# Fewer, longer load runs and a last product that also sums the partial sums, in a streaming Poisson loss

## The chip, the cores and the metric

The kernel runs on one core of one Trainium2 chip. The metric is the device time of one execution in microseconds (us), median of several runs. All runs told of here were at a granted clock of 1.0. About 1.4 us of each time lies outside the span that the profile shows (84.78 against 83.4 for the profiled run of the kernel before).

## The reference

```python
# log_input, target: 1024 x 4096, float32
loss = np.exp(log_input) - target * log_input
return np.mean(loss, axis=-1)
```

33.55 MB are read and 4 KB written. A partition holds 8 consecutive rows of 4096 columns (16 KB a row), so 4 rows of one partition are 64 KB in one piece of memory.

## The kernel before

ScalarE takes the exp of x row by row and sums it, DVE multiplies t and x and sums that. All loads go out on one queue, x and t in turn: two rows (32 KB per partition) at a time for rows 0 to 5, row 6 alone, row 7 in seven pieces, so that little is left to compute after the last bytes. The first six loads are issued at once; the rest wait until the first pair of rows is done.

```python
TAIL = [("x", 32), ("t", 32), ("x", 24), ("t", 12), ("t", 12), ("x", 6), ("t", 5), ("x", 2), ("t", 3)]
...
for g in range(groups - 1):                       # groups = 4
    loads += [("x", 2 * d * g, 2 * d), ("t", 2 * d * g, 2 * d)]
...
# ScalarE, after its last exp: join the six partial sums of row 7
join(2 * n_whole, n_parts, most, len(t_work) - 1).then_inc(join_done, 1)
...
    nc.vector.wait_ge(landed[x_load], 16)
    nc.vector.tensor_tensor_reduce(               # the last one: accum_out = rest
        out=t_buf[...], in0=t_buf[...], in1=x_buf[...], op0=ALU.mult, op1=ALU.add, accum_out=accum, ...
    ).wait_op(landed[i], 16, "sem-ge").then_inc(prod_done, 1)
nc.vector.wait_ge(join_done, nb)
nc.vector.tensor_tensor(                          # the closing sum
    out=all_loss[:, nb - 1 : nb], in0=most, in1=rest, op=ALU.add
).wait_op(prod_done, len(t_work), "sem-ge").then_inc(loss_done, 1)
nc.sync.dma_start(out=out_v, in_=all_loss).wait_op(loss_done, 1, "sem-ge")...
```

## Time and profile before

| | before |
|---|---|
| time, median (range) | 84.19 us (84.17 to 84.25, 6 runs) |
| span of the profiled run | 83.4 us (its time: 84.78) |
| last load landed | 81.09 us |
| from there to the issue of the output | 0.81 us |
| from the output's issue to the end | 1.45 us |

The times count from the first issue of a load. The profiled run was 0.6 us slower than the timed ones; the slow packets that the prediction finds in its DMA records (its rival 2) are the likely reason. The lines of the page, of the table of stretches and of the timeline's end are shown in the prediction.

### The profile page before, as it was taken

Reading aid. Unit: us, or ns where it says so; the run is one execution under the profiler, and the core shown is the slowest. Engines: PE = TensorE matmul, PEld = TensorE weight load, DVE = VectorE, ACT = ScalarE, POOL = GpSimd, SP = SyncE. Lnnn points to the kernel's source line nnn. Section 1 sums busy time; section 2 is a strip of 40 time slices with the busy share of each in tenths; the row PEclk is TensorE's granted clock in tenths of the full one; section 3 lists DMA queues with packets and bytes.
Section 4 is the critical chain, followed back from the end, with each engine's and each line's share of the span. In section 5 each row is a group of like instructions: output and inputs, shape, how many; then the busy total and the mean of one; then the engine's idle time right before and its main releaser. Section 6 shows DMA issues by size and latency. Waiting matters only on the chain.

```text
span 83.4 us, 145 instructions
## 1 busy us (share of the span) xinstructions
DVE 35.9 (43%) x23; ACT 33.7 (40%) x37; POOL 0.2 (0%) x4
## 2 busy tenths in 40 slices
DVE  0000000000599960000099991000069995994992
ACT  0050029993001008998000102999300496019371
POOL 0000000000000000000000000000000000000000
DMA  8799969998996996995996997999799999999960
GB/s 252 330 425 503 487 283 487 503 409 346 503 503 252 503 503 252 503 503 252 503 503 267 487 503 330 425 503 440 314 448 432 409 472 387 430 407 422 395 224 2
DMA packets 2304, 33.56 MB, mean 403 GB/s; under 512 B 384, under 2 KB 640, under 8 KB 1152
## 3 DMA queue, kind: packets, MB, share of 16 engines
q1 hardware_dynamic: 2304, 33.56, 95.8%
HBM read 33.55 MB, written 0.00 MB: 403 GB/s over the span
## 4 chain that ended last, share of the span: by engine, by line
DMA 81%; DVE 7%; issue 6%; SPq 4%
DMA t_buf<-in_target_dram 81%; DVE t_buf L169 6%; SPq L114 4%; DVE parts L169 0%; DVE all_loss L180 0%; DVE rest L169 0%; SPq L113 0%
## 5 line engine op out<-in xcount | busy, mean ns | idle before, releaser
L169 DVE CUSTOM_DVE_ANT_0 t_buf<-t_buf,x_buf 128x4096 f32<-128x4096 f32 (+3 forms) x11 | 35.6, 3260 | 46.0 <-DMA t_buf<-in_target_dram 45.8
L139 ACT ACTIVATE e_dump<-x_buf 128x4096 f32<-128x4096 f32 (+3 forms) x10 | 29.0, 2901 | 23.3 <-DMA x_buf<-in_log_input_dram 23.1
L123 ACT ACTIVATE join_dump<-parts 128x2 f32<-128x2 f32 (+1 forms) x8 | 1.6, 204 | 20.5 <-DVE parts L169 20.2
L139 ACT ACT_TABLE_LOAD x1 | 1.3, 1283 | 4.0 <-PEq L48 4.0
L139 ACT ACTIVATION_READ_ACCUMULATOR e_dump<-x_buf 128x1 f32 x10 | 1.9, 186 | 0.0
L123 ACT ACTIVATION_READ_ACCUMULATOR join_dump<-parts 128x1 f32 x8 | 1.5, 186 | 0.0
L169 DVE DVE_READ_ACCUMULATOR2_ANT parts<- 128x1 f32 x10 | 0.8, 82 | 0.0
L180 DVE TENSOR_TENSOR all_loss<-most,rest 128x1 f32<-128x1 f32 x1 | 0.2, 159 | 0.0
L206 POOL MEMSET const-bfloat16-1.0<- 128x1 bf16 x1 | 0.1, 102 | 0.0
L206 POOL MEMSET const-uint8-127<- 128x1 uint8 x1 | 0.1, 101 | 0.0
L206 POOL MEMSET const-float32-0.0<- 128x1 f32 x1 | 0.1, 99 | 0.2 <-issue 0.2
L206 POOL MEMSET const-float32-1.0<- 128x1 f32 x1 | 0.1, 98 | 0.0
L169 DVE DVE_READ_ACCUMULATOR2_ANT rest<- 128x1 f32 x1 | 0.1, 82 | 0.0
## 6 DMA issues: line engine op xcount, KB each, us to landing
x_buf<-in_log_input_dram SPq DMA_DIRECT2D x3, 4096.0 KB, 30.6
t_buf<-in_target_dram SPq DMA_DIRECT2D x3, 4096.0 KB, 40.2
x_buf<-in_log_input_dram SPq DMA_DIRECT2D x1, 2048.0 KB, 35.5
t_buf<-in_target_dram SPq DMA_DIRECT2D x1, 2048.0 KB, 40.0
x_buf<-in_log_input_dram SPq DMA_DIRECT2D x1, 1536.0 KB, 43.2
t_buf<-in_target_dram SPq DMA_DIRECT2D x2, 768.0 KB, 45.3
x_buf<-in_log_input_dram SPq DMA_DIRECT2D x1, 384.0 KB, 46.5
t_buf<-in_target_dram SPq DMA_DIRECT2D x1, 320.0 KB, 46.6
```

Of the source, the lines that this page charges most:

```text
L114: dma = nc.sync.dma_start(out=buf[:, in_slot(lo, w)], in_=src[:, lo : lo + w])
L123: return nc.scalar.activation(out=join_dump[:, first : first + count], in_=parts[:, first : first + count], func=ACT_F.Copy, scale=inv_d, ...
L139: nc.scalar.activation(out=e_dump[:, col : col + w], in_=x_buf[:, in_slot(lo, w)], func=ACT_F.Exp, bias=0.0, scale=1.0, accum_out=parts[:, ...
L169: nc.vector.tensor_tensor_reduce(out=t_buf[:, in_slot(lo, w)], in0=t_buf[:, in_slot(lo, w)], in1=x_buf[:, in_slot(lo, w)], scale=-inv_d if ...
L180: nc.vector.tensor_tensor(out=all_loss[:, nb - 1 : nb], in0=most, in1=rest, op=ALU.add).wait_op(prod_done, len(t_work), "sem-ge").then_inc ...
L206: nc = _bacc.Bacc("TRN2", target_bir_lowering=False, num_devices=1)
```

## The change

Rows 0 to 3 of x go in one load of 64 KB per partition, then those of t; rows 4 and 5 keep 32 KB. That saves 2 loads and 16 packets for each DMA engine. The six partial sums of row 7 are laid behind the last columns of t, with -1 in the same places behind x, so that the last product, six columns wider, adds them up; the join on ScalarE and the closing sum go.

```diff
-    for g in range(groups - 1):
-        loads += [("x", 2 * d * g, 2 * d), ("t", 2 * d * g, 2 * d)]
+    for first, rows in ((0, 4), (4, 2), (6, 1)):
+        loads += [("x", first * d, rows * d), ("t", first * d, rows * d)]
...
+        if what == "x" and lo in (6 * d, 7 * d):          # buffers of rows 0 and 3 are used again
+            free = 1 if lo == 6 * d else 4
+            nc.sync.wait_ge(exp_done, free)
+            nc.sync.wait_ge(prod_done, free)
...
+    nc.gpsimd.memset(big["x"][:, 4 * d : 4 * d + n_parts], -1.0).then_inc(ones_done, 1)
...
-    join(2 * n_whole, n_parts, most, len(t_work) - 1).then_inc(join_done, 1)
...
+            nc.vector.wait_ge(ones_done, 1)
+            nc.vector.wait_ge(landed[i], 16)
+            nc.vector.wait_ge(prod_done, n_t - 1)
+            nc.vector.tensor_tensor_reduce(
+                out=place("t", lo, w + n_parts),
+                in0=place("t", lo, w + n_parts),
+                in1=place("x", lo, w + n_parts),
+                scale=-inv_d, ...
+                accum_out=all_loss[:, last_row : last_row + 1],
+            ).wait_op(exp_done, n_x, "sem-ge").then_inc(loss_done, 1)
-    nc.vector.wait_ge(join_done, nb)
-    nc.vector.tensor_tensor(
-        out=all_loss[:, nb - 1 : nb], in0=most, in1=rest, op=ALU.add
-    ).wait_op(prod_done, len(t_work), "sem-ge").then_inc(loss_done, 1)
```

More of the change, by code (lines that the diff above doesn't have):

```diff
@@ L8 @@
 F32 = mybir.dt.float32
-TAIL = [
-    ("x", 32), ("t", 32), ("x", 24), ("t", 12), ("t", 12), ("x", 6), ("t", 5), ("x", 2), ("t", 3),
-]
+TAIL = [("x", 24), ("t", 12), ("t", 12), ("x", 6), ("t", 5), ("x", 2), ("t", 3)]
 def before_first_barrier(nc, instructions):
@@ L54 @@
     inv_d = 1.0 / d
-    slots = 3
-    groups = nb // 2
+    last_row = nb - 1
     x_v = log_input.rearrange("(p b) d -> p (b d)", b=nb)
@@ L63 @@
     loads = []
-    for g in range(groups - 1):
-        loads += [("x", 2 * d * g, 2 * d), ("t", 2 * d * g, 2 * d)]
-    at = {"x": 2 * d * (groups - 1), "t": 2 * d * (groups - 1)}
+    for first, rows in ((0, 4), (4, 2), (6, 1)):
+        loads += [("x", first * d, rows * d), ("t", first * d, rows * d)]
+    at = {"x": last_row * d, "t": last_row * d}
     for what, w in TAIL:
@@ L81, with place, part @@
     x_work, t_work = work("x"), work("t")
-    n_whole = nb - 1
-    assert all(w == d for _, w, _ in x_work[:n_whole] + t_work[:n_whole])
-    x_buf = nc.alloc_sbuf_tensor("x_buf", [P, slots * 2 * d], F32).ap()
-    t_buf = nc.alloc_sbuf_tensor("t_buf", [P, slots * 2 * d], F32).ap()
-    e_dump = nc.alloc_psum_tensor("e_dump", [P, d], F32).ap()
-    n_parts = len(x_work) - n_whole + len(t_work) - n_whole - 1
-    parts = nc.alloc_sbuf_tensor("parts", [P, 2 * n_whole + n_parts], F32).ap()
-    join_dump = nc.alloc_sbuf_tensor("join_dump", [P, 2 * n_whole + n_parts], F32).ap()
-    most = nc.alloc_sbuf_tensor("most", [P, 1], F32).ap()
-    rest = nc.alloc_sbuf_tensor("rest", [P, 1], F32).ap()
+    n_x, n_t = len(x_work), len(t_work)
+    n_parts = n_x - last_row + n_t - last_row - 1
+    big = {
+        "x": nc.alloc_sbuf_tensor("x_big", [P, 4 * d + n_parts], F32).ap(),
+        "t": nc.alloc_sbuf_tensor("t_big", [P, 4 * d + n_parts], F32).ap(),
+    }
+    mid = {
+        "x": nc.alloc_sbuf_tensor("x_mid", [P, 2 * d], F32).ap(),
+        "t": nc.alloc_sbuf_tensor("t_mid", [P, 2 * d], F32).ap(),
+    }
+    def place(what, lo, w):
+        row = lo // d
+        if 4 <= row < 6:
+            return mid[what][:, lo - 4 * d : lo - 4 * d + w]
+        if row >= 6:
+            lo -= (6 if row == 6 else 4) * d
+        return big[what][:, lo : lo + w]
+    e_dump = nc.alloc_psum_tensor("e_dump", [P, d], F32).ap()
+    parts = nc.alloc_sbuf_tensor("parts", [P, 2 * last_row], F32).ap()
+    join_dump = nc.alloc_sbuf_tensor("join_dump", [P, 2 * last_row], F32).ap()
     all_loss = nc.alloc_sbuf_tensor("all_loss", [P, nb], F32).ap()
-    def in_slot(lo, w):
-        lo %= slots * 2 * d
-        return slice(lo, lo + w)
+    def part(k):
+        return big["t"][:, 4 * d + k : 4 * d + k + 1]
     landed = [nc.alloc_semaphore(f"landed{i}") for i in range(len(loads))]
@@ L103 @@
     join_done = nc.alloc_semaphore("join_done")
+    ones_done = nc.alloc_semaphore("ones_done")
     loss_done = nc.alloc_semaphore("loss_done")
@@ L109, with join @@
     for i, (what, lo, w) in enumerate(loads):
-        buf, src = (x_buf, x_v) if what == "x" else (t_buf, t_v)
-        if lo == 2 * d * slots and what == "x":
-            nc.sync.wait_ge(exp_done, 2)
-            nc.sync.wait_ge(prod_done, 2)
-        dma = nc.sync.dma_start(out=buf[:, in_slot(lo, w)], in_=src[:, lo : lo + w])
+        if what == "x" and lo in (6 * d, 7 * d):
+            free = 1 if lo == 6 * d else 4
+            nc.sync.wait_ge(exp_done, free)
+            nc.sync.wait_ge(prod_done, free)
+        src = x_v if what == "x" else t_v
+        dma = nc.sync.dma_start(out=place(what, lo, w), in_=src[:, lo : lo + w])
         dma.then_inc(landed[i], 16)
-        if lo + w <= 2 * d * slots:
+        if lo < 6 * d:
             early.append(dma.ins)
     before_first_barrier(nc, early)
-    def join(first, count, accum, prods):
+    nc.gpsimd.memset(big["x"][:, 4 * d : 4 * d + n_parts], -1.0).then_inc(ones_done, 1)
+    def join(row, exps):
         nc.scalar.wait_ge(exp_done, exps)
-        return nc.scalar.activation(
-            out=join_dump[:, first : first + count],
-            in_=parts[:, first : first + count],
+        nc.scalar.activation(
+            out=join_dump[:, 2 * row : 2 * row + 2],
+            in_=parts[:, 2 * row : 2 * row + 2],
             func=ACT_F.Copy,
             scale=inv_d,
-            accum_out=accum,
-        ).wait_op(prod_done, prods, "sem-ge")
-    exps = 0
-    for lo, w, i in x_work:
+            accum_out=all_loss[:, row : row + 1],
+        ).wait_op(prod_done, row + 1, "sem-ge").then_inc(join_done, 1)
+    for k, (lo, w, i) in enumerate(x_work):
         row, col = lo // d, lo % d
-        if row >= 2 and col == 0:
-            join(2 * (row - 2), 2, all_loss[:, row - 2 : row - 1], row - 1).then_inc(join_done, 1)
-        if col == 0 and row > 0:
-            nc.scalar.wait_ge(exp_done, exps)
-        k = 2 * row if row < n_whole else 2 * n_whole + exps - n_whole
+        if col == 0 and row >= 2:
+            join(row - 2, k)
+        elif col == 0 and row == 1:
+            nc.scalar.wait_ge(exp_done, k)
         nc.scalar.activation(
             out=e_dump[:, col : col + w],
-            in_=x_buf[:, in_slot(lo, w)],
+            in_=place("x", lo, w),
             func=ACT_F.Exp,
@@ L144 @@
             scale=1.0,
-            accum_out=parts[:, k : k + 1],
+            accum_out=parts[:, 2 * row : 2 * row + 1] if row < last_row else part(k - last_row),
         ).wait_op(landed[i], 16, "sem-ge").then_inc(exp_done, 1)
-        exps += 1
-        if row == n_whole and col == 0:
-            row -= 1
-            join(2 * row, 2, all_loss[:, row : row + 1], row + 1).then_inc(join_done, 1)
-    join(2 * n_whole, n_parts, most, len(t_work) - 1).then_inc(join_done, 1)
-    needs = {}
-    for lo, w, i in x_work:
-        needs[lo + w] = i
+        if col == 0 and row == last_row:
+            join(row - 1, k + 1)
@@ L157 @@
     for j, (lo, w, i) in enumerate(t_work):
         row = lo // d
-        last = j == len(t_work) - 1
-        if last:
-            accum = rest
-        elif row < n_whole:
-            accum = parts[:, 2 * row + 1 : 2 * row + 2]
-        else:
-            k = 2 * n_whole + len(x_work) - n_whole + j - n_whole
-            accum = parts[:, k : k + 1]
-        x_load = next(needs[end] for end in sorted(needs) if end >= lo + w)
-        nc.vector.wait_ge(landed[x_load], 16)
-        nc.vector.tensor_tensor_reduce(
-            out=t_buf[:, in_slot(lo, w)],
-            in0=t_buf[:, in_slot(lo, w)],
-            in1=x_buf[:, in_slot(lo, w)],
-            scale=-inv_d if last else -1.0,
-            scalar=0.0,
-            op0=ALU.mult,
-            op1=ALU.add,
-            accum_out=accum,
-        ).wait_op(landed[i], 16, "sem-ge").then_inc(prod_done, 1)
@@ L179 @@
-    nc.vector.wait_ge(join_done, nb)
-    nc.vector.tensor_tensor(
-        out=all_loss[:, nb - 1 : nb], in0=most, in1=rest, op=ALU.add
-    ).wait_op(prod_done, len(t_work), "sem-ge").then_inc(loss_done, 1)
+        x_load = next(ix for a, wx, ix in x_work if a + wx >= lo + w)
+        nc.vector.wait_ge(landed[x_load], 16)
+        if j < n_t - 1:
+            nc.vector.tensor_tensor_reduce(
+                out=place("t", lo, w),
+                in0=place("t", lo, w),
+                in1=place("x", lo, w),
+                scale=-1.0,
+                scalar=0.0,
+                op0=ALU.mult,
+                op1=ALU.add,
+                accum_out=parts[:, 2 * row + 1 : 2 * row + 2]
+                if row < last_row
+                else part(n_x - last_row + j - last_row),
+            ).wait_op(landed[i], 16, "sem-ge").then_inc(prod_done, 1)
+        else:
+            nc.vector.wait_ge(ones_done, 1)
+            nc.vector.wait_ge(landed[i], 16)
+            nc.vector.wait_ge(prod_done, n_t - 1)
+            nc.vector.tensor_tensor_reduce(
+                out=place("t", lo, w + n_parts),
+                in0=place("t", lo, w + n_parts),
+                in1=place("x", lo, w + n_parts),
+                scale=-inv_d,
+                scalar=0.0,
+                op0=ALU.mult,
+                op1=ALU.add,
+                accum_out=all_loss[:, last_row : last_row + 1],
+            ).wait_op(exp_done, n_x, "sem-ge").then_inc(loss_done, 1)
@@ L185 @@
+    nc.sync.wait_ge(join_done, last_row)
     nc.sync.dma_start(out=out_v, in_=all_loss).wait_op(loss_done, 1, "sem-ge").then_inc(
@@ L187 @@
     )
-    used = landed + [exp_done, prod_done, join_done, loss_done]
+    used = landed + [exp_done, prod_done, join_done, ones_done, loss_done]
     nc.sync.sem_clear(range(used[0].num, out_done.num))
```

## The prediction

> **What bounds the kernel now.** I read the page from the top, then the chain of waits, then the timeline from 51 us on, then the DMA records by size. First the page: engine shares, the DMA row, packets and queue.
>
> ```profile
> span 83.4 us, 145 instructions
> DVE 35.9 (43%) x23; ACT 33.7 (40%) x37; POOL 0.2 (0%) x4
> ...
> DMA packets 2304, 33.56 MB, mean 403 GB/s; under 512 B 384, under 2 KB 640, under 8 KB 1152
> ...
> q1 hardware_dynamic: 2304, 33.56, 95.8%
> ...
> DMA 81%; DVE 7%; issue 6%; SPq 4%
> ```
>
> The two working engines are idle more than half the span, while the 16 DMA engines are busy 95.8% of it. The count also tells what a packet is: 15 loads x 128 partitions is 1920, the output's 128 makes 2048, and 16 transfers x 16 completion writes is 256, in all 2304. So every contiguous run of one partition is one packet, the largest so far 32 KB. The last row says that the chain that ended last is DMA for 81%, with a short DVE tail. How full the stream is, and whether it slows beside compute, a table of four stretches shows (columns: DVE, ACT, POOL busy; clock; DMA share; GB/s):
>
> ```profile
> 22.00:30.00 8.00, 8.00 (x3) 0.30 (x2) 0.00 (x0) 1.00 1.08 459
> 31.00:41.00 10.00, 0.00 (x0) 7.60 (x6) 0.00 (x0) 1.00 1.02 426
> 42.00:51.00 9.00, 8.39 (x4) 0.30 (x2) 0.00 (x0) 1.00 1.07 451
> 52.00:61.00 9.00, 0.00 (x0) 7.09 (x6) 0.00 (x0) 1.00 1.02 437
> ```
>
> The reader is to see a DMA share of 1 in every stretch (a packet is counted where it starts, hence the values above 1): no queue ever runs dry. Then the end of the timeline:
>
> ```profile
> 78.46 1.76 DVE L169 CUSTOM_DVE_ANT_0 t_buf<-t_buf,x_buf 128x1536 f32<-128x1536 f32 x1
> 79.44 0.81 ACT L139 ACTIVATE e_dump<-x_buf 128x768 f32<-128x768 f32 x1 [1.51 <-DMA x_buf<-in_log_input_dram]
> ...
> 80.28 0.82 DVE L169 CUSTOM_DVE_ANT_0 t_buf<-t_buf,x_buf 128x640 f32<-128x640 f32 x1
> 80.64 0.39 ACT L139 ACTIVATE e_dump<-x_buf 128x256 f32<-128x256 f32 x1 [0.27 <-DMA x_buf<-in_log_input_dram]
> 80.96 0.19 ACT L139 ACTIVATION_READ_ACCUMULATOR e_dump<-x_buf 128x1 f32 x1
> 81.03 0.08 DVE L169 DVE_READ_ACCUMULATOR2_ANT parts<- 128x1 f32 x1
> 81.11 0.56 DVE L169 CUSTOM_DVE_ANT_0 t_buf<-t_buf,x_buf 128x384 f32<-128x384 f32 x1
> 81.24 0.21 ACT L123 ACTIVATE join_dump<-parts 128x6 f32<-128x6 f32 x1
> 81.36 0.19 ACT L123 ACTIVATION_READ_ACCUMULATOR join_dump<-parts 128x1 f32 x1
> 81.60 0.08 DVE L169 DVE_READ_ACCUMULATOR2_ANT rest<- 128x1 f32 x1
> 81.72 0.16 DVE L180 TENSOR_TENSOR all_loss<-most,rest 128x1 f32<-128x1 f32 x1
> 81.90 0.35 SPq L185 DMA_DIRECT2D out_dram<-all_loss  x1
> ```
>
> The last load lands at 81.09 (its completion records); the last product starts at 81.11, is done with its read-out at 81.68, one small sum follows to 81.88, and the output's issue and landing take the rest to 83.4. The ScalarE join of the six partial sums (81.24 to 81.55) lies beside the last product and ends 0.13 us before it. So the time is: 81.1 us of stream, 0.8 us of tail, 1.5 us of output. Only the first two are touched.
>
> **What the Trainium skill says.** "DMA: Bandwidth & Descriptors", section "Why small descriptors are slow (HBM only)": a packet carries a fixed overhead of about 3 cycles, and each operation 32 bytes of metadata, so larger runs pay it less often. The trace agrees that there is a fixed part: the records give a median of 611 ns for a 16 KB packet and 1213 ns for 32 KB, so 2 x 611 - 1213 = 9 ns are fixed, and the rest is 16384 B in 602 ns, or 27.2 GB/s an engine. The same page, "Where 436 GB/s comes from", puts the ceiling of the 16 engines at 435 GB/s; 16 x 27.2 agrees, and the stretch from 52 us shows 437. Bigger packets can therefore win the fixed nanoseconds and nothing more. "VectorE: DVE Perf Modes", section "The DRAIN you can't avoid", says a read after a write on the same engine needs a semaphore; that is why the new last product waits for the product before it. Before, the closing sum waits so, and starts 0.03 us after the read-out ended. Fourth, the DMA page's "How a descriptor splits into AXI transactions" has a transfer that starts off a 256-byte boundary pay extra beats; no row of this kernel shows it, since its buffers are whole powers of two. I use it for a risk below.
>
> **The change part by part.** *Loads.* Rows 0 to 3 go as 2 loads of 8 packets an engine in place of 4: 32 packets of 32 KB an engine become 16 of 64 KB, and 15 loads become 13. Estimated from the two medians, a 64 KB packet takes 9 + 2408 = 2417 ns; two of 32 KB take 2426. Saved: 16 x 9 ns = 0.144 us, plus 2 completion writes of 9 ns (their record) = 0.018 us. Sum 0.16 us, all on the path, since the stream is. Rows 4 and 5, row 6 and the seven pieces of row 7 keep their sizes.
>
> *Order of work.* The coarser loads delay compute early. x of rows 0 to 3 lands at about 21.6, t at about 41.0 (two times 19.35 us in place of 4 landings ending 41.59 in a trace that had some slow packets, see below). DVE then does four products of 4.35 us (pitch 26.08 minus 21.73) and is done at about 58.4. t of rows 4 and 5 lands near 61.0, as before. So DVE has about 2.5 us to spare and meets the rest as before. ScalarE now has exps of rows 2 and 3 held by the joins of rows 0 and 1 until about 46 and 50, and row 5's exp ends about 63; x of row 6 lands at about 66. Spare: about 3 us.
>
> *Gates.* Row 6 may be issued after product 1, at about 45.5, while rows 4 and 5 keep the queue full to 61. Row 7 may be issued after product 4, at about 58.4; seven issues at 0.45 us (the pitch from 30.98 to 31.94) end near 62, and row 6 keeps the queue full to 70.8. Neither gate starves the stream. Before, one issue hung 8.6 us at 33.70 with nine loads outstanding; at 58.4 nine is again reached only by the last ones, and they are not due before 80.
>
> *Tail.* Removed: the six-column join (beside other work, worth nothing) and the closing sum with its wait, 81.68 to 81.88 = 0.20 us. Added: six columns on the last product. The slope is (4423 - 558) / (4096 - 384) = 1.04 ns a column, so 6 ns. Added too: it can start only when the previous product's sum (81.11) and the last exp's (81.15) are counted, and a separate wait comes before it. ScalarE shows what that costs: it saw the last exp's count at 81.16 and started the join at 81.24, 0.08 us. I take the same for DVE from 81.12, so it starts at 81.20 in place of 81.11: 0.09 us lost. Net: 0.20 - 0.09 - 0.01 = 0.10 us won. The memset of the ones is about 0.1 us on idle POOL at the start, worth nothing; the wait on the joins at the output is long satisfied.
>
> Sum: 84.19 - 0.16 - 0.10 = 83.93 us.
>
> **The rivals.** (1) *A 64 KB run is cut into two packets anyway.* Nothing before shows one over 32 KB. Then only the 0.02 us of completions and the tail are won: 84.07. (2) *The stream's slow packets change.* In the profiled execution, packets begun between 20 and 53 us took up to 1.38 us in place of 1.213; summed, 0.8 us an engine, while those before and after were exact. It isn't DVE or ScalarE: both also run beside exact packets (ScalarE 12 to 19, DVE 61 to 78). The profiled execution took 84.78 us where the timed ones took 84.19, so most of this probably isn't in the timed runs. If it depends on run length or on outstanding loads, the new kernel could win or lose up to 0.8 us: 83.2 to 84.7. (3) *Misaligned destinations.* The new buffers carry six spare columns (24 bytes), so the buffers behind them may start off a round boundary. If each packet pays a beat or two, it is a few ns x some 50 packets, under 0.3 us; if every transaction paid, up to 1/8 of the affected half to three quarters of the stream, and the time would be several us longer, 88 or more. Against it: allocators usually round up. I give it 4%. (4) *The tail becomes a new wait.* If DVE's separate waits cost 0.2 us and not 0.08, the tail wins nothing: 84.0. (5) *A gate starves the stream.* The margins of 15 and 12 us say no.
>
> **Range and chances.** Rivals 1 and 4 move the time by 0.15 upward at most; the timed runs of before agree within 0.06; rival 2 gives both sides some tenths. I put the time at 83.93 us, with 83.5 to 84.4 to hold it 8 times in 10. Faster by over 2% would need less than 82.5, which is below what a full stream at 27.2 GB/s an engine allows once start, tail and output are added (77.1 + 1.0 + 0.6 for the slow first packet, + 0.8 + 1.5, + 1.4 outside the span, which is 84.78 - 83.4, = 82.4, with no packet overhead at all): 2%. Within 2%: 93%. Slower by over 2%: 5%, nearly all of it rival 3.
>
> **What would show it.** Right: 256 fewer data packets and 32 fewer completions (2304 becomes 2016, as 2 x 128 and 2 x 16 go), 64 KB packets at about 2.42 us, a first DVE product near 41, DVE idle again before 61, a last product of 128x390 that starts about 0.09 us after the one before it ends and is followed by the output's issue within 0.12 us. Wrong: 32 KB packets still there for rows 0 to 3; packets longer than their bytes at 27.2 GB/s for whole buffers; a DMA share under 0.95 around 46, 61 or 70 us; a last product that waits more than 0.15 us.

## The result, and the profile after

The changed kernel took 84.17 us (median; 84.06 to 84.65, 6 runs) beside 84.19 before. The ratio was 1.0004, with a 95% interval of 0.9981 to 1.0028. A ratio is the mean time of one kernel's fast runs over that of the other's of the same rounds, so it isn't quite the ratio of the medians. Two more measurements of the same kernel, as controls of the experiments, gave 0.9993 and 0.9988. Nothing to speak of was won.

The page of the changed kernel: engine shares, packets, queue, and the shares of the chain that ended last.

```profile
span 82.7 us, 136 instructions
DVE 35.6 (43%) x22; ACT 33.2 (40%) x35; POOL 0.3 (0%) x5
...
DMA packets 2016, 33.56 MB, mean 406 GB/s; under 512 B 352, under 2 KB 608, under 8 KB 1120
...
q1 hardware_dynamic: 2016, 33.56, 95.6%
...
DMA 72%; DVE 14%; issue 10%; SPq 2%; DVEq 0%
```

2304 packets became 2016, the 288 that were foretold: a 64 KB run is one packet. In the DMA records its median is 2418 ns. The span is 0.6 us shorter, but the timed runs don't show that: this profiled run took 84.06 us and had 0.25 us of slow packets an engine, that of before took 84.78 and had 0.93. The end of the timeline (start, duration, engine, line, operation; then idle time and what ended it):

```profile
80.28 0.19 ACT L152 ACTIVATION_READ_ACCUMULATOR e_dump<-x_big 128x1 f32 x1
80.35 0.08 DVE L169 DVE_READ_ACCUMULATOR2_ANT t_big<- 128x1 f32 x1
80.67 0.57 DVE L185 CUSTOM_DVE_ANT_0 t_big<-t_big,x_big 128x390 f32<-128x390 f32 x1 [0.24 <-ACT e_dump L152]
81.16 0.09 DVE L185 DVE_READ_ACCUMULATOR2_ANT all_loss<- 128x1 f32 x1
81.27 0.35 SPq L198 DMA_DIRECT2D out_dram<-all_loss  x1
```

The last load landed at 80.41. The closing sum is gone, but DVE now stands idle for 0.24 us ahead of the last product, where before it stood 0.01. The page names the last exp as the one that ended that wait, yet its read-out was over at 80.46, 0.21 us earlier. The chain of waits shows what lay between (DVEq is DVE's sequencer, "issue" a gap in which nothing is waited for that the profile shows):

```profile
80.43 0.01 issue
80.44 0.05 DVEq L183
80.49 0.05 issue
80.54 0.05 DVEq L184
80.59 0.09 issue
80.67 0.57 DVE t_big L185
```

Two wait instructions, one after the other. The code has four waits ahead of the product; in the trace they are packed two to an instruction: the landing and the ones (L183), the product before and the landing of x (L184). All four were fulfilled by 80.44, but the sequencer takes about 0.1 us for each. From the last landing to the issue of the output it is now 0.86 us, in place of 0.81.

| | before | after |
|---|---|---|
| median | 84.19 us | 84.17 us |
| nominal time of data and completion packets, per engine | 78.23 | 78.09 |
| slow packets in the profiled run, per engine, first 5 us left out | 0.93 | 0.25 |
| last load landed, profiled run | 81.09 | 80.41 |
| last landing to output issue | 0.81 | 0.86 |

(Nominal: each packet's usual time from the DMA records, 9 ns for a completion, 611, 1213 and 2418 ns for 16, 32 and 64 KB, and so on for the smaller sizes of row 7, summed and divided by 16. Slow packets: what the records took beyond that. The 0.93 takes in all packets after the first 5 us, the 0.8 of the prediction only those between 20 and 53 us.)

### The profile page after: what moved, and what is told of

Read it like the earlier page. It is cut to its first block, busy times and chain, and to the rows that moved or that the text cites. A ratio compares the mean times of both kernels' runs of the same rounds, so it can differ in the third digit from the quotient of the medians.

```text
span 82.7 us, 136 instructions
## 1 busy us (share of the span) xinstructions
DVE 35.6 (43%) x22; ACT 33.2 (40%) x35; POOL 0.3 (0%) x5
## 2 busy tenths in 40 slices
DMA packets 2016, 33.56 MB, mean 406 GB/s; under 512 B 352, under 2 KB 608, under 8 KB 1120
## 3 DMA queue, kind: packets, MB, share of 16 engines
q1 hardware_dynamic: 2016, 33.56, 95.6%
## 4 chain that ended last, share of the span: by engine, by line
DMA 72%; DVE 14%; issue 10%; SPq 2%; DVEq 0%
DMA t_big<-in_target_dram 72%; DVE t_big L169 13%; SPq L126 2%; DVE t_big L185 1%; DVE parts L169 0%; DVEq L184 0%; DVEq L183 0%; DVEq L167 0%; SPq L124 0%; DVE all_loss L185 0%
## 5 line engine op out<-in xcount | busy, mean ns | idle before, releaser
L169 DVE CUSTOM_DVE_ANT_0 t_big<-t_big,x_big 128x4096 f32<-128x4096 f32 (+2 forms) x8 | 26.2, 3308 | 43.4 <-DMA t_big<-in_target_dram 43.2
L152 ACT ACTIVATE e_dump<-x_big 128x4096 f32<-128x4096 f32 (+3 forms) x8 | 21.8, 2730 | 23.9 <-DMA x_big<-in_log_input_dram 23.6
L138 ACT ACTIVATE join_dump<-parts 128x2 f32<-128x2 f32 x7 | 1.4, 203 | 20.4 <-DVE parts L169 20.3
L169 DVE CUSTOM_DVE_ANT_0 t_mid<-t_mid,x_mid 128x4096 f32<-128x4096 f32 x2 | 8.8, 4422 | 2.0 <-DMA t_mid<-in_target_dram 2.0
L152 ACT ACTIVATE e_dump<-x_mid 128x4096 f32<-128x4096 f32 x2 | 7.1, 3568 | 0.0
L152 ACT ACTIVATION_READ_ACCUMULATOR e_dump<-x_big 128x1 f32 x8 | 1.5, 186 | 0.0
L185 DVE CUSTOM_DVE_ANT_0 t_big<-t_big,x_big 128x390 f32<-128x390 f32 x1 | 0.6, 568 | 0.2 <-ACT e_dump L152 0.2
```

The lines of the kernel that those rows point to most:

```text
L138: nc.scalar.activation(out=join_dump[:, 2 * row : 2 * row + 2], in_=parts[:, 2 * row : 2 * row + 2], func=ACT_F.Copy, scale=inv_d, accum_o ...
L152: nc.scalar.activation(out=e_dump[:, col : col + w], in_=place("x", lo, w), func=ACT_F.Exp, bias=0.0, scale=1.0, accum_out=parts[:, 2 * ro ...
L169: nc.vector.tensor_tensor_reduce(out=place("t", lo, w), in0=place("t", lo, w), in1=place("x", lo, w), scale=-1.0, scalar=0.0, op0=ALU.mult ...
L185: nc.vector.tensor_tensor_reduce(out=place("t", lo, w + n_parts), in0=place("t", lo, w + n_parts), in1=place("x", lo, w + n_parts), scale= ...
```

## The experiments

All outputs are right. The theories, named as in the expectations: A, the new tail loses because its waits pass one after another, while the big runs win by the fixed cost of packets; B, the tail won as predicted and the loads lost it; C, a big run at the start of the stream starts it later.

**The two halves apart.** First the changed kernel unaltered, as a control.

> The changed kernel unaltered, as a control beside the others. Its trace ended the loads at 80.41 us, with the last product starting 0.26 us later. Both theories: 84.1 to 84.25 us, last landing to output issue 0.86 us.

84.22 us, ratio to before 0.9993 (0.9977 to 1.001), last landing to output issue 0.86 us. Then only the tail:

```diff
-    for first, rows in ((0, 4), (4, 2), (6, 1)):
+    for first, rows in ((0, 2), (2, 2), (4, 2), (6, 1)):
```

> The changed kernel with rows 0 to 3 again in two runs of 32 KB; buffers, gates and the new last product stay. Theory A (the new tail's waits pass one after another and cost more than the closing sum they replace): last landing to output issue 0.86 us in place of 0.81 before, so 0.05 us slower than before, 84.2 to 84.3. Theory B (the tail won its 0.10 us as I predicted and the loads lost it): 0.71 us, 84.09. Theory C (a big run costs a slow start): the first packets' excess over their nominal time falls from 0.68 to about 0.58 us per engine.

84.28 us, ratio 1.0006 (0.9985 to 1.0027); last landing to output issue 0.86 us. And only the loads, with join and closing sum as before, in the new buffers (shortened: the line with # stands for the last product as it was before):

```diff
-            nc.vector.wait_ge(ones_done, 1)
-            nc.vector.wait_ge(landed[i], 16)
-            nc.vector.wait_ge(prod_done, n_t - 1)
+            # last product 384 wide, accum_out=rest, wait_op(landed[i], 16)
+    nc.vector.wait_ge(join_done, nb)
+    nc.vector.tensor_tensor(out=all_loss[:, nb - 1 : nb], in0=most, in1=rest, op=ALU.add)...
```

> The changed kernel's loads and buffers with the tail of before (join on ScalarE, closing sum on DVE). Theory A (9 ns fixed per packet, tail a loss): last landing to output issue 0.81 us, 0.16 us faster than before and 0.05 faster than the changed kernel: 84.03. Theory B (tail won): slower than the changed kernel by 0.10. Theory C (big runs start slower by 0.1 us): 84.1 with a start excess of 0.68 us per engine.

84.19 us, ratio 0.9987 (0.9972 to 1.0001); last landing to output issue 0.81 us. The end of its timeline:

```profile
80.39 0.08 DVE L178 DVE_READ_ACCUMULATOR2_ANT parts<- 128x1 f32 x1
80.49 0.56 DVE L191 CUSTOM_DVE_ANT_0 t_big<-t_big,x_big 128x384 f32<-128x384 f32 x1
...
81.09 0.16 DVE L202 TENSOR_TENSOR all_loss<-most,rest 128x1 f32<-128x1 f32 x1
81.28 0.35 SPq L207 DMA_DIRECT2D out_dram<-all_loss  x1
```

The landing was at 80.46 and the product began 0.02 us later: with its one open wait in the instruction itself, it starts at once. B falls: the tail is the same 0.86 or 0.81 us whatever the loads, and the new one is the slower by 0.05. The load half came out 0.11 us faster than before by its ratio, an interval that just reaches 1, and the control against the tail-only kernel says the same (0.9993 over 1.0006). By the medians it is only 0.04 and 0.06 us, since a few long runs (84.48 and 84.50 of before, 84.69 of tail only) weigh on the means. C's number wasn't met: the start excess of the tail-only kernel was 0.69, not 0.58. I had read it wrongly, see below.

**The waits.** If the two wait instructions are the cost, one wait in the product itself must take it away. The last load, the last exp and the product before the last count up one semaphore: 16 + 1 + 1.

```diff
+    all_in = nc.alloc_semaphore("all_in")      # last load +16, last exp +1, product before last +1
-            nc.vector.wait_ge(landed[i], 16)
-            nc.vector.wait_ge(prod_done, n_t - 1)
+            nc.vector.wait_ge(exp_done, n_x - 1)     # long fulfilled when DVE gets there
+            nc.vector.wait_ge(prod_done, n_t - 2)
...
-            ).wait_op(exp_done, n_x, "sem-ge").then_inc(loss_done, 1)
+            ).wait_op(all_in, 18, "sem-ge").then_inc(loss_done, 1)
```

> The changed kernel, but the last load, the last exp and the product before last all count up one semaphore, so the last product waits once, for 18. Theory A (two separate waits in a row cost 0.2 us): the last product starts about 0.05 us after the last exp's read-out in place of 0.21, last landing to output issue 0.70 us, 0.16 us faster than the changed kernel: about 84.0. Rival (the start is held by data coming back to the same engine, not by the waits): still 0.86 us, no change.

84.08 us, ratio 0.9974 (0.9958 to 0.9989); 0.70 us from landing to output issue. Its timeline:

```profile
80.39 0.19 ACT L153 ACTIVATION_READ_ACCUMULATOR e_dump<-x_big 128x1 f32 x1
80.44 0.08 DVE L170 DVE_READ_ACCUMULATOR2_ANT t_big<- 128x1 f32 x1
80.60 0.57 DVE L186 CUSTOM_DVE_ANT_0 t_big<-t_big,x_big 128x390 f32<-128x390 f32 x1
81.20 0.35 SPq L199 DMA_DIRECT2D out_dram<-all_loss  x1
```

The exp's read-out ends at 80.57 by the unrounded records and the product starts 0.03 us later. The data still come back to the same engine, so the rival falls. Two wait instructions stand ahead of the product here too, but they were over at 80.07, 0.43 us before the last landing: what costs is a wait instruction that comes after the last events. Then the dose the other way, two more waits for loads that landed long ago:

```diff
             nc.vector.wait_ge(prod_done, n_t - 1)
+            nc.vector.wait_ge(landed[i - 1], 16)
+            nc.vector.wait_ge(landed[i - 2], 16)
```

> The changed kernel with two more waits ahead of the last product, for loads that landed long ago. Two waits share one wait instruction, so this is one instruction more. Theory A (each wait instruction in the row costs about 0.1 us even when satisfied): last landing to output issue 0.96 us, the time 0.1 us longer. Rival (only unsatisfied waits cost): 0.86 us, no change.

84.38 us beside 84.18 of its control (the means of the six runs each are 0.14 us apart, but the intervals of the two ratios to before, 1.0005 and 0.9988, overlap, so the traces are the firmer ground); 0.98 us from landing to output issue. The chain now has three wait instructions, 0.097 us apart:

```profile
80.57 0.05 DVEq L184
80.62 0.05 issue
80.67 0.05 DVEq L185
80.72 0.05 issue
80.76 0.05 DVEq L186
80.81 0.08 issue
80.89 0.57 DVE t_big L187
```

The series 0.70, 0.86, 0.98 us for none, two and three wait instructions behind the last events settles the tail.

**The runs.** The control on the second chip:

> The changed kernel once more, as the control on this chip. 84.1 to 84.25 us, last landing to output issue 0.86 us.

84.18 us, ratio 0.9988 (0.997 to 1.0007), 0.86 us. Against it a large lever on packet size:

```diff
-    for first, rows in ((0, 4), (4, 2), (6, 1)):
+    for first, rows in [(r, 1) for r in range(7)]:
```

> The changed kernel with rows 0 to 6 each in a run of its own of 16 KB, 21 loads in place of 13: the packet cost taken with a large lever. Theory A (9 ns fixed per packet and per completion write): data and completions by their nominal times are 0.42 + 0.14 + 0.07 = 0.63 us per engine more than in the changed kernel, all of it on the path, so about 84.8 us. Rival (packet size costs nothing that shows, the stream's end is set by slow packets and the start): within 0.15 us of the changed kernel, 84.2.

84.66 us, ratio to before 1.0044 (1.0025 to 1.0062), 0.48 us over its control, and the last load landed at 80.96 in place of 80.55. So smaller runs do cost, but by less than theory A had it, 0.63. The DMA records show why the estimate was too large. The durations of an engine's packets, summed, are longer than the time they all took: by 0.42 us an engine in the control's trace, by 0.67 here. Over 117 and 189 records an engine that is 3.6 ns a record in both. Records of neighbouring packets overlap, so the 9 ns that I read from two durations aren't all time on the path. The pace is read from ends instead: I took the mean end of the packets that complete each engine's second and eighth 64 KB, a stretch without slow packets. Per 64 KB it is 2.4153 us with one packet (changed kernel), 2.4198 with two (tail only) and 2.4312 with four (this kernel). From two packets to one the gain is 4.5 ns for a packet saved, the few completions in the stretch included.

The other end of the stream shows the second half of the matter. In the first of the two lines below both kernels have moved the same 8.4 MB when the waiting engine starts (x and t of two rows, or x of four), in the second the same 16.8 MB. First the tail-only kernel, with 32 KB runs, then the control, with 64 KB runs:

```profile
21.73 4.42 DVE L169 CUSTOM_DVE_ANT_0 t_big<-t_big,x_big 128x4096 f32<-128x4096 f32 x1 [21.73 <-DMA t_big<-in_target_dram]
...
41.17 4.43 DVE L169 CUSTOM_DVE_ANT_0 t_big<-t_big,x_big 128x4096 f32<-128x4096 f32 x1 [10.66 <-DMA t_big<-in_target_dram]
```

```profile
21.88 3.59 ACT L152 ACTIVATE e_dump<-x_big 128x4096 f32<-128x4096 f32 x1 [17.66 <-DMA x_big<-in_log_input_dram]
...
41.23 4.43 DVE L169 CUSTOM_DVE_ANT_0 t_big<-t_big,x_big 128x4096 f32<-128x4096 f32 x1 [41.23 <-DMA t_big<-in_target_dram]
```

By packets alone the second should be ahead by 0.08 and 0.16 us at these two points. It is behind by 0.15 and 0.06. This pair lies at the far end: in the changed kernel's own trace the two starts are 21.73 and 41.07. Over all traces: 8.4 MB were in at 21.70 to 21.75 in the four with 32 KB runs at the start and at 21.71 to 21.89 (mean 21.81) in the eight with 64 KB. Already the first 64 KB of an engine (mean end over the engines) were in at 4.20 to 4.25 with 16 or 32 KB runs and at 4.27 to 4.34 with 64 KB. That is C after all, about 0.08 us. My expectation had missed it because it compared the excess of the first packets alone, while the engines' first starts, which vary by 0.2 us, trade against it.

Does it follow the run, and nothing else? Two kernels split one side each, on the one-counter tail:

```diff
-    for first, rows in ((0, 4), (4, 2), (6, 1)):
+    loads += [("x", 0, 2 * d), ("x", 2 * d, 2 * d), ("t", 0, 4 * d)]      # x_pairs
+    # or: loads += [("x", 0, 4 * d), ("t", 0, 2 * d), ("t", 2 * d, 2 * d)]  # t_pairs
+    for first, rows in ((4, 2), (6, 1)):
```

> The one-counter kernel unaltered, as the control on this chip, and a second measurement of the version that seems to beat both. 84.0 to 84.1 us, last landing to output issue 0.70 us; the first 64 KB of an engine are in at about 4.30 us, as in all six traces with a 64 KB run at the start (4.28 to 4.34).

84.00 us, ratio to before 0.9967 (0.9943 to 0.9991), 0.70 us; first 64 KB in at 4.27.

> The one-counter kernel, but x of rows 0 to 3, with which the stream starts, goes in two runs of 32 KB; t keeps its one of 64 KB. Theory A (a 64 KB run as the first packet costs 0.09 us at the start, whatever comes later): the first 64 KB of an engine are in at 4.22 us on the mean in place of 4.30, as in the three traces with 32 KB runs; 8 packets and one completion more give back 0.05, so the time is 0.04 us shorter than the control or the same. Rival (the late first 64 KB is chance or comes from the buffers): 4.30.

84.02 us, ratio 0.9975 (0.9946 to 1.0004); first 64 KB in at 4.24, and t of row 3 landed at 41.10 in place of 41.14 in the control.

> The reverse: x of rows 0 to 3 in one run of 64 KB, t in two of 32 KB. Theory A: the first 64 KB of an engine are in at 4.30 us, the start keeps its cost, and the smaller packets of t take 2.420 us per 64 KB in place of 2.415: 0.05 us longer than the control. Rival: 4.22.

84.14 us, ratio 0.998 (0.9956 to 1.0005); first 64 KB in at 4.31, t of row 3 landed at 41.21. The order is theory A's, but x_pairs moved only 0.03 of the 0.08 against this control, and 0.07 against t_pairs; the times tell nothing apart between x_pairs and the control. So the late start goes with a 64 KB run as first packet in every trace, with a size of 0.08 us on the mean of all traces and of 0.03 and 0.07 in these two comparisons; its mechanism stays open.

Last, the loads of before under the one-counter tail (the edits of the one-counter and tail-only kernels together):

> The loads of the kernel before (runs of 32 KB) with the last product waiting once on one counter. Theory A: last landing to output issue 0.70 us, 0.16 us per engine more of packets than with the big runs: 0.11 us faster than before, 84.1, and slower than the one-counter kernel by 0.15. Rival (big runs win nothing): equal to the one-counter kernel, 84.05.

84.09 us, ratio 0.9975 (0.9957 to 0.9993), beside 0.9974 and 0.9967 of the one-counter kernel; 0.72 us from landing to output issue. The gain is in the tail; the long runs add nothing that these runs resolve.

**What stays open.** The slow packets. After the first 5 us they summed to 0.21 to 0.27 us an engine in all eight traces that begin with a 64 KB run, and to 0.45 to 0.93 in the five that begin with smaller ones. That would favour the long runs. But two profiled runs of the second group were far slower than the median of the timed runs (before 84.78 against 84.19, x_pairs 84.57 against 84.02), so the traces overstate it, and x_pairs had its slow packets at rows 4 to 6, long after the split rows. Of the timed runs, 8 of 63 that begin with smaller runs were more than 0.2 us over their kernel's median in that measurement, and 2 of 48 that begin with 64 KB: too few to tell. The slow packets may be what is left of the load half's 0.11 us; no run here shows what causes them.

**The version that beats both** is the one-counter kernel: 84.08 and 84.00 us in two measurements on two chips, 0.26% and 0.33% faster than before by the ratios, both intervals below 1. Beside the changed kernel on the same chip it is 0.9974 over 0.9993, or 0.19% faster; these two intervals overlap, but the means of the six runs each are 0.16 us apart, as much as the tails in the two traces.

## Why the prediction was right or wrong

The forecast, 83.93 us in a range of 83.5 to 84.4 and 93% for "within 2%", held: 84.17. That says little, since the range had room for no gain at all and for twice the gain promised. The prediction was right about the bound. The stream sets the end, the gates of rows 6 and 7 starve nothing (DMA share 95.6%), the first product moved to 41.07 and DVE stood idle again before row 4 (1.96 us, where 2.5 were foretold), all without effect. Of the rivals, the cut 64 KB run and the misaligned destinations didn't come: 64 KB packets took 2418 ns, where 2417 were estimated. (The costs given for misaligned rows were estimates from the beats that the cited page gives; no run here has rows that are known to be misaligned. Two small slips did no harm: the pitch of the issues is 0.48 us and not 0.45, as 30.98 to 31.94 holds two, and the old buffers were 96 KB, not a power of two.)

But the sum promised 0.26 us, and 0.02 came by the medians (0.06 and 0.10 by the ratios of the two controls, all three intervals around 1). Two of its terms were mis-sized.

- *Tail.* The step that failed is "Net: 0.20 - 0.09 - 0.01 = 0.10 us won". The closing sum did go and the six columns were nearly free (0.568 us for 390 columns, 0.558 for 384). But the start of the last product moved from 0.02 to 0.26 us after the landing, and its wait of 0.24 us is one of the prediction's own signs of being wrong (more than 0.15). I had priced one separate wait, from ScalarE (0.08), where the code puts several ahead of the product. They became two wait instructions of about 0.1 us each, in a row, behind the last events. The tail lost 0.05. Rival 4 had named this, with 0.2 us for the waits, and was right. A page of the skill could have led me there: "Perfetto Trace Analysis", section "Identifying Dependency Chains", says that waits on several engines can become instructions of their own ahead of the waiting one, and "Advanced Engine Details and Errata", section "Network/Comms", gives 50 to 100 ns for reading a semaphore from a sequencer. The trace fits that for waits with two conditions, 50 ns each and 0.097 us from one to the next; a wait with one condition took 21 ns in the trace of before, which is less.
- *Loads.* The step "Saved: 16 x 9 ns = 0.144 us, plus 2 completion writes ... Sum 0.16 us, all on the path" failed in two places. A saved packet is worth 4.5 ns of pace and not 9, since packet records overlap: 16 x 4.5 = 0.07 us, completions about included. And with 64 KB runs at the start the first 64 KB come some 0.08 us later (0.03 and 0.07 in the two comparisons made for it), which takes that back. By the landing of row 3 the changed kernel and its controls (41.05 to 41.22) were level with the 32 KB kernels that had next to no slow packets by then (41.13 and 41.15). The timed load half, 0.11 us, isn't resolved from zero.

So the expected gain went to two wait instructions (0.15 us) and to a fixed cost that was half of what it looked like and was spent at the start.

## What to carry to other kernels

Ahead of the instruction that ends a kernel, count the wait instructions behind the last event: each cost about 0.1 us on DVE here even when fulfilled, so let the last events count up one semaphore and wait for the total in the instruction itself. Read a packet's fixed cost from the pace of the stream, not from two durations, and check that the first bytes don't come later with the longer run. In a stream that sets 80 of 84 us and whose 16 engines were busy over 95% of the span, merging packets from 32 KB up won nothing that these runs resolve.

## What the Trainium skill lacked or had wrong

- "Perfetto Trace Analysis" tells that waits become instructions of their own, but not their price ahead of a DVE instruction: 50 ns and a gap of as much for one with two conditions (21 ns with one condition, in the trace of before), 0.097 us pitch, three in a row 0.28 us later than none.
- "DMA: Bandwidth & Descriptors", "Why small descriptors are slow (HBM only)", tells of a fixed cost per packet but not that durations of packets overstate it: 9 ns by duration, 4.5 ns by pace between 32 and 64 KB runs.
- The same page: I found no word that a stream that begins with 64 KB runs has its first 64 KB later than one with 32 KB runs: 4.27 to 4.34 us against 4.20 to 4.25.
- I found no page that tells of packets that run up to some 14% long for tens of us with no engine of the core to blame (before: 1.38 us in place of 1.213), 0.2 to 0.9 us an engine in a run.
